# A hybrid encoder layer on one core: Hyena tiles read four and two ahead, output projection in fp16 parts

## The chip, the core and the metric

The kernel runs on one core of a Trainium2 chip. A core has a matrix engine (TensorE, PE in the profile), a vector engine (VectorE, DVE), a scalar engine (ScalarE, ACT), a general one (GpSimd, POOL) and an engine that issues most of the transfers here (SyncE, SP), each with its own instruction row, worked off in order. An instruction waits until those it depends on have signalled, and everything behind it on its engine waits with it. Working memory on the chip is SBUF (128 partitions); TensorE writes its results to PSUM, from which the other engines take them. The metric is the time of one launch in microseconds on the device; smaller is better.

## What is computed

One layer over two inputs, a prompt of 512 rows and a sample of 2048 rows, each row 1024 wide: 2560 rows, or 20 chunks of 128 rows. A normalised input is projected by `w_in`; three groups of heads (mLSTM, retention, Hyena) give 512 columns each; the 1536 mixed columns are projected back by `w_out` and added to the input, and a last RMSNorm follows.

```python
u = jnp.einsum('bld,de->ble', rmsnorm(x, norm_g[layer]), w_in[layer])
y_ml = mlstm_branch(...)       # 4 heads, both directions, chunks of 128
y_rt = retention_branch(...)   # 4 heads, both directions
y_hy = hyena_branch(...)       # z = x1*long_conv(v); z = x2*long_conv(z); z*silu(hy_z)
mixed = jnp.concatenate([y_ml, y_rt, y_hy], axis=-1)
x = x + jnp.einsum('ble,ed->bld', mixed, w_out[layer])
return rmsnorm(x, final_g)
```

`long_conv` is a convolution over the whole length through an FFT of twice the length; in the kernel each FFT is two rounds of small matmuls with a pass through memory between.

## The kernel before

The program has five stages in time. First a front part (normalisation, the Hyena projections). Then two streams that are merged: the Hyena stream, and a stream of the other input projections followed by retention. Then mLSTM, four heads, each in blocks of 512 rows. Then the output projection with the final norm.

**The merge.** `merge` takes generators with a total cost each and lets the one run next that has the smallest share of its cost done. A step yields its cost, and through `lag` also how much of the other stream's work has to pass before its own next step. A scheduler reorders on each engine what the generators emit, by its own estimate of times; the order that results is fixed when the kernel is built.

**The Hyena stream** is `stage_a0`, `freq(0)`, `inv_a(0)`, `freq(1)`, `inv_a(1)`. Tiles are 128 x 512 float32, 256 KB, from a pool of 18 buffers (`hb`). `stage_a0` loads `X` tiles two ahead and multiplies them (L921). `inv_a` works through 20 tiles twice: `load` brings two tiles of `Z`, `load_x` brings `X` (and for the second order `hyg`, a gate), `mid` multiplies `Z` (L1028), DVE multiplies by `X` (L1029), and for the second order POOL multiplies by the gate (L1033) and SP writes the result to `ymix` (L1036), the buffer of the mixed columns in memory. Per turn the order is `mid` of tile i, `X` of tile i+1, `Z` of tile i+2.

**The projections** of the other stream and of mLSTM are L554 and L544: fp16 matmuls, since `split_w` has scaled each weight matrix by a power of two (`scale_w`: a maximum on DVE, L348; a tiny matmul for the maximum over partitions, L358; a few small DVE steps) and cut it into a high and a low fp16 part (ACT L526, DVE L527).

**The output projection** works on two parts as well, but in float32r: `split` (L369 on ACT, L370 on DVE) cuts a tensor into a rounded part and the rest. The 1536 rows of `w_out` come in six groups of 256 rows (`load_wout`, L1211, two buffers); `split_wout` cuts one group and loads the next. Groups 0 to 3 are cut in the blocks of mLSTM's last head (`block_left`). `out_product` (L1287) makes 72 matmuls of 128 x 512 per row chunk: 12 column blocks, three products (high by high, high by low, low by high), two halves of the output. `turn_mixed` transposes the activations first (L1275, 12 transposes into three PSUM tiles, each split by L369 and L370). The first row chunk is done early: `early_load` reads its mixed columns, and `early_rows` runs beside the last mLSTM block, with groups 4 and 5 cut at steps 1 and 6 of its product. `final` then does chunks 1 to 19: product with the next chunk's transposes in its middle (step 5 of 12), addition of the input (L1343), square sum (L1350 on ACT), power (L1352 on POOL), scaling (L1354), store. The last block's own matmuls are L1438 and L1534 to L1539.

## Time and profile before

| what | value |
|---|---|
| median of three runs | 2651.07 us (2650.94 to 2654.84) |
| the profiled execution | 2648.68 us |
| its span, first to last instruction | 2646.9 us |
| granted TensorE clock, mean | 0.988 |
| TensorE (PE) busy | 2557.2 us, 97% |
| VectorE (DVE) busy | 1338.3 us, 51% |
| ScalarE (ACT) busy | 1053.7 us, 40% |
| GpSimd (POOL) busy | 493.9 us, 19% |
| moved by DMA | 321.30 MB, 121 GB/s over the span |
| chain that ended last | PE 78%, DMA 6%, ACT 4%, DVE 4% |

The share of busy time is an average over stages; where TensorE is busy all the time, only its own work counts, and where it waits, the thing it waits for. The clock is 1 where TensorE runs at 2.4 GHz and 0.5 where it runs at 1.2 GHz.

### The profile page before, as it was taken

To read this page: it belongs to the slowest core of one execution; us is meant where nothing else is said; L and a number is where in the kernel's file an instruction comes from. 1 tells how busy PE (TensorE), PEld (TensorE's weight loads), DVE (VectorE), ACT (ScalarE), POOL (GpSimd) and SP (SyncE) were. 2 spreads that over 40 slices of the span, in tenths; PEclk is the share of its full clock that TensorE was granted. 3 is DMA by queue.
4 is the path that set the end of the run, shared out by engine and by line. 5 is a ranking of instruction groups with operands and counts; after the bars stand their busy time and mean duration, and the time that the engine had idled before them with its cause. 6 is when DMAs were issued, how large, how long until landed. Compare 5 with 4: busy or idle time off the path is not lost.

```text
span 2646.9 us, 45607 instructions
## 1 busy us (share of the span) xinstructions
PE 2557.2 (97%) x17830; PEld 1770.2 (67%) x17830; DVE 1338.3 (51%) x3070; ACT 1053.7 (40%) x2030; POOL 493.9 (19%) x647
## 2 busy tenths in 40 slices
PE   7999979999999999999999979999999999899998
PEld 5565543444446777777777747787887777788887
DVE  6875635665554434545444444565556645522222
ACT  6455646442233333423333323555445545411111
POOL 0103312331011122322232341111111111100000
PEclk9999989999999999999999989999999999999999
DMA  6233377564454665434333782222121322322331
GB/s 207 84 99 108 98 220 252 167 187 127 126 160 128 207 198 160 126 100 132 116 104 97 226 228 65 52 66 61 37 64 42 89 73 59 133 102 95 111 104 48
DMA packets 238049, 321.30 MB, mean 121 GB/s; under 512 B 22755, under 2 KB 125947, under 8 KB 237833
## 3 DMA queue, kind: packets, MB, share of 16 engines
q1 hardware_dynamic: 237752, 318.11, 39.8%
q8 instruction: 141, 2.31, 0.4%
q14 instruction: 76, 0.61, 0.1%
q0 software_dynamic: 80, 0.26, 0.0%
HBM read 205.41 MB, written 112.89 MB: 120 GB/s over the span
## 4 chain that ended last, share of the span: by engine, by line
PE 78%; DMA 6%; ACT 4%; DVE 4%; issue 1%; SPq 1%; POOL 1%; DVEq 0%; POOLq 0%; ACTq 0%
PE ps L554 27%; PE ps L544 13%; PE ps L1287 13%; PE ps L948 6%; DMA rb<-rowd 3%; PE ps L983 3%; PE ps L1028 2%; PE ps L921 1%; PE ps L1639 1%; DMA wraw<-in_w_in 1%; PE ps L693 1%; PE ps L1438 1%; PE ps L1275 1%; PE ps L1698 1%; PE ps L846 1%
## 5 line engine op out<-in xcount | busy, mean ns | idle before, releaser
L554 PE MATMUL ps<-whi,h 128*128 128x256 f16 (+2 forms) x6080 | 913.7, 256 | 0.0
L554 PEld LDWEIGHTS <-h 128*128 128x128 f16 x9120 | 776.0, 98 | 150.0 <-issue 69.5
L554 PE MATMUL ps<-wlo,h 128*128 128x256 f16 (+2 forms) x3040 | 734.6, 256 | 0.0
L544 PE MATMUL ps<-h,whi 128*128 128x512 f16 x1600 | 484.9, 383 | 4.0 <-ACT whi L526 4.0
L544 PE MATMUL ps<-h,wlo 128*128 128x512 f16 x800 | 305.0, 381 | 0.0
L544 PEld LDWEIGHTS <-whi 128*128 128x128 f16 x1600 | 151.1, 99 | 212.8 <-issue 63.0
L1287 PE MATMUL ps<-h,yh 128*128 128x512 f32 x760 | 210.6, 396 | 1.6 <-ACT yh L369 1.6
L948 PE MATMUL ps<-hb,cB 128*64 128x512 f32 x640 | 165.9, 605 | 0.2 <-DMA hb<-F 0.2
L1287 PEld LDWEIGHTS ps<-h,yh 128*128 128x128 f32 x760 | 141.6, 188 | 33.7 <-ACT yh L369 1.9
L668 POOL TENSOR_TENSOR acc<-acc,win 128x512 f32<-128x512 f32 x80 | 107.2, 1340 | 201.4 <-ACT win L667 196.2
L544 PEld LDWEIGHTS <-wlo 128*128 128x128 f16 x800 | 78.7, 98 | 94.7 <-issue 4.9
L1618 POOL TENSOR_TENSOR m<-raw,tb 128x256 f32<-128x256 f32 x80 | 72.3, 904 | 336.2 <-ACT raw L1615 273.2
L1287 PE MATMUL ps<-h,yl 128*128 128x512 f32 x380 | 120.9, 395 | 0.0
L1615 ACT ACTIVATE raw<-ps,winv 128x256 f32<-128x256 f32 x80 | 37.8, 473 | 167.5 <-PE ps L554 98.9
L662 DVE TENSOR_TENSOR f<-ps,win 128x512 f32<-128x512 f32 x80 | 55.0, 688 | 88.7 <-PE ps L378 66.1
L813 DVE SCALAR_TENSOR_TENSOR cv<-u,sw,cv 128x512 f32<-128x512 f32 x120 | 98.1, 838 | 1.1
L527 DVE SCALAR_TENSOR_TENSOR wlo<-wraw,wsc,whi 128x512 f16<-128x512 f32 (+2 forms) x116 | 82.6, 749 | 22.8 <-ACT whi L526 21.6
L1637 ACT ACTIVATE vw<-va,rtv 128x128 f32<-128x128 f32 x144 | 51.9, 398 | 100.4 <-PE ps L1639 100.0
L948 PEld LDWEIGHTS ps<-hb,cB 128*64 128x64 f32 x640 | 41.5, 136 | 73.2 <-issue 60.6
L348 DVE TENSOR_REDUCE wam<-wraw 128x1 f32<-128x2048 f32 (+2 forms) x29 | 60.0, 2069 | 60.0 <-DMA wraw<-in_w_in 60.0
L1343 DVE TENSOR_TENSOR xt<-xt,ps 128x512 f32<-128x512 f32 x40 | 25.8, 684 | 126.9 <-PE ps L1287 126.9
L971 POOL TENSOR_TENSOR hb<-hb,hb 128x512 f32<-128x512 f32 x40 | 50.9, 1273 | 185.5 <-DVE hb L970 176.3
(318 smaller groups left out, 4045.8 us busy)
## 6 DMA issues: line engine op xcount, KB each, us to landing
F<-fo SPq DMA_DIRECT2D x160, 128.0 KB, 2.4
Sg<-hb SPq DMA_DIRECT2D x80, 256.0 KB, 2.3
hb<-F SPq DMA_DIRECT2D x80, 256.0 KB, 4.3
hb<-Sg SPq DMA_DIRECT2D x80, 256.0 KB, 5.1
Z<-hb SPq DMA_DIRECT2D x80, 256.0 KB, 3.5
hb<-Z SPq DMA_DIRECT2D x80, 256.0 KB, 3.7
rb<-rowd SPq DMA_DIRECT2D x80, 256.0 KB, 5.1
wraw<-in_w_in SPq DMA_DIRECT2D x36, 512.0 KB, 5.8
```

The lines of the kernel that those rows point to most:

```text
L348: self.nc.vector.tensor_reduce(am[:, 0:1], src, axis=AX.XY if len(src.shape) == 3 else AX.X, op=ALU.max, apply_absolute_value=True)
L527: v = nc.vector.scalar_tensor_tensor(lo[:, k], raw[:, k], s, hi[:, k], op0=ALU.mult, op1=ALU.subtract)
L544: nc.tensor.matmul(out, w[x][:, k, wc:wc + 128], self.hT[b][y][:, k], start=(k == 0 and i == 0), stop=(k == 7 and i == 2))
L554: nc.tensor.matmul(out, self.hT[b][x][:, k, c * 128:(c + 1) * 128], w[y][:, k, wc:wc + n], start=(k == 0 and i == 0), stop=(k == 7 and i = ...
L662: nc.vector.tensor_tensor(out=f, in0=ps, in1=win, op=ALU.mult)
L668: nc.gpsimd.tensor_tensor(out=acc, in0=acc, in1=win, op=ALU.add)
L813: nc.vector.scalar_tensor_tensor(d, u[:, t:t + 512], w(t), d, op0=ALU.mult, op1=ALU.add)
L948: nc.tensor.matmul(ps[half[h]], Cs[i][:, 128 * h + 64 * r:128 * h + 64 * r + 64], src[h], start=True, stop=True)
L983: nc.tensor.matmul(pz[h], c[half[h], 256 + 128 * r:384 + 128 * r], y[r][half[h]], start=(r == 0), stop=(r == 1))
L1028: nc.tensor.matmul(ps[64 * h:64 * h + 64], self.ai[L][:, 128:192], z[h], start=True, stop=True)
L1287: self.nc.tensor.matmul(self.pss[n], a[p], w[q][:, n * 512:(n + 1) * 512], start=(k == 0 and i == 0), stop=(k == 11 and i == 2))
L1618: nc.gpsimd.tensor_tensor(out=m, in0=raw[:, :, ::-1], in1=sin[:, c:c + 2], op=ALU.mult)
```

## The change

In the Hyena stream `stage_a0` loads four tiles ahead instead of two; `inv_a` loads both `Z` and `X` (and the gate) two tiles ahead, and per turn does `mid` first, then the loads, then for the first order `back`. The yielded costs and lags are others, and the stream's share in the merge is 295 instead of 275.

In the output projection both operands become fp16 parts. Each weight group gets a power-of-two scale (`scale_w`) and is cut in two instructions of 128 x 2048; the inverse scales are kept in `wog`. Per row chunk `mixed_parts` finds for each row the largest value times the inverse scale over the six column groups, makes a power-of-two factor of it, and cuts the activations into two fp16 parts in 12 instructions of 256 columns, before the transposes. `turn_mixed` then makes 24 fp16 transposes and copies three PSUM tiles of 128 x 1024. The addition of the input multiplies the product by the row's inverse factor. Groups 4 and 5 are cut in `early_load`. In `final` the parts of the next chunk are made at step 0 of the product, its transposes stand at step 8.

```diff
-                    self.drain(self.merge((self.chain(self.stage_a0(), self.freq(0), self.inv_a(0), self.freq(1), self.inv_a(1)), 275 * W3),
+                    self.drain(self.merge((self.chain(self.stage_a0(), self.freq(0), self.inv_a(0), self.freq(1), self.inv_a(1)), 295 * W3),
...
+        self.ident16 = self.T(cp, [128, 128], "ident16", F16)
+        nc.vector.tensor_copy(self.ident16, self.ident)
...
             st[i] = self.hx(0, L, j)
 
         n = len(seq)
-        load(0)
-        load(1)
-        for i in range(n + 1):
-            if i:
-                L, j = seq[i - 1]
-                self.stage_a(L, 0, j, st.pop(i - 1))
-            if i + 2 < n:
-                load(i + 2)
-            yield self.lag(0.86, 1.5)
+        for i in range(4):
+            load(i)
+        yield self.lag(0.0, 9.0)
+        for i in range(n):
+            L, j = seq[i]
+            self.stage_a(L, 0, j, st.pop(i))
+            if i + 4 < n:
+                load(i + 4)
+            yield self.lag(1.0, 0.5)
 
...
             self.stage_a(L, 1, j, st.pop(i))
 
         n = len(seq)
-        load(0)
-        yield self.lag(0.0, 5.0)
-        for i in range(-1, n + 1):
+        for i in range(2):
+            load(i)
+            load_x(i)
+        yield self.lag(0.0, 7.0)
+        for i in range(n + 1):
+            if i < n:
+                mid(i)
+            if i + 2 < n:
+                load(i + 2)
+                load_x(i + 2)
             if o == 0 and i >= 1:
                 back(i - 1)
-            if 0 <= i < n:
-                mid(i)
-            if i + 1 < n:
-                load_x(i + 1)
-            if i + 2 < n:
-                load(i + 2)
-            yield self.lag(1.71 if o == 0 else 0.86, LI)
+            yield self.lag(1.0 if o else 2.0, 1.5)
 
...
 
     def split_wout(self, i, hi, lo):
 
-        for k in range(2):
-            self.split(hi[k], lo[k], self.wraw[:, k])
+        nc = self.nc
+        if i == 0:
+            self.wog = self.T(self.cp, [128, 6], "wog")
+        s, inv = self.scale_w(self.wp, self.wraw)
+        nc.vector.tensor_copy(self.wog[:, i:i + 1], inv)
+        nc.scalar.activation(hi, self.wraw, AF.Copy, scale=s)
+        nc.vector.scalar_tensor_tensor(lo, self.wraw, s, hi, op0=ALU.mult, op1=ALU.subtract)
         self.wout[i] = hi, lo
         self.load_wout(i + 1)
 
     def block_left(self, h, b):
 
         if h == 3:
-            hi, lo = (self.T(self.hp, [128, 2, D], "h", F32R, bufs=10) for _ in range(2))
+            hi, lo = (self.T(self.hp, [128, 4, D], "h", F16, bufs=10)[:, 0:2] for _ in range(2))
             if b == 0:
                 self.load_wout(0)
-            self.split_next = lambda: self.split_wout(b, *([x[:, k] for k in range(2)] for x in (hi, lo)))
+            self.split_next = lambda: self.split_wout(b, hi, lo)
             if b < 4:
                 self.split_next()
 
...
         self.want(*MlHead.first_w(0))
         self.flush()
 
-    def turn_mixed(self, yt, yh, yl):
-
-        for y, hi, lo in zip(yt, yh, yl):
-            ps = self.ps()
-            for i in range(4):
-                self.nc.tensor.transpose(ps[:, i * 128:(i + 1) * 128], y[:, i * 128:(i + 1) * 128], self.ident)
-            self.split(hi, lo, ps)
-
-    def out_product(self, yh, yl, halves=((0, 1),)):
+    def mixed_parts(self, pool, yt, yp):
+
+        nc = self.nc
+        am = self.T(pool, [128, 8], "yam")
+        ie = self.T(pool, [128, 4], "yie", I32)
+        sc = self.T(pool, [128, 2], "ysc")
+        fs = self.T(pool, [128, 6], "yfs")
+        for q, y in enumerate(yt):
+            nc.vector.tensor_reduce(am[:, 2 * q:2 * q + 2], y.rearrange("p (g c) -> p g c", g=2), axis=AX.X, op=ALU.max, apply_absolute_value=True)
+        nc.vector.tensor_tensor(out=am[:, 0:6], in0=am[:, 0:6], in1=self.wog, op=ALU.mult)
+        nc.vector.tensor_reduce(am[:, 6:7], am[:, 0:6], axis=AX.X, op=ALU.max)
+        nc.vector.tensor_scalar(ie[:, 0:1], am[:, 6:7].bitcast(I32), 23, None, op0=ALU.logical_shift_right)
+        nc.vector.tensor_scalar(ie[:, 1:2], ie[:, 0:1], 15, 250, op0=ALU.max, op1=ALU.min)
+        nc.vector.tensor_scalar(ie[:, 2:3], ie[:, 1:2], -1, 268, op0=ALU.mult, op1=ALU.add)
+        nc.vector.tensor_scalar(ie[:, 3:4], ie[:, 1:2], -14, None, op0=ALU.add)
+        nc.vector.tensor_scalar(sc.bitcast(I32), ie[:, 2:4], 23, None, op0=ALU.logical_shift_left)
+        nc.vector.tensor_scalar(fs, self.wog, sc[:, 0:1], None, op0=ALU.mult)
+        for q, (y, p) in enumerate(zip(yt, yp)):
+            for g in range(2):
+                f, c = fs[:, 2 * q + g:2 * q + g + 1], slice(256 * g, 256 * g + 256)
+                nc.scalar.activation(p[:, 0, c], y[:, c], AF.Copy, scale=f)
+                nc.vector.scalar_tensor_tensor(p[:, 1, c], y[:, c], f, p[:, 0, c], op0=ALU.mult, op1=ALU.subtract)
+        return sc[:, 1:2]
+
+    def turn_mixed(self, parts, out):
+
+        nc = self.nc
+        for q, (y, o) in enumerate(zip(parts, out)):
+            ps = self.psum.tile([128, 2, 512], F16, tag="ps", name=self.nm("ps"))
+            for x in range(2):
+                for i in range(4):
+                    nc.tensor.transpose(ps[:, x, i * 128:(i + 1) * 128], y[:, x, i * 128:(i + 1) * 128], self.ident16)
+            if q == 1:
+                nc.vector.tensor_copy(o, ps)
+            else:
+                nc.scalar.activation(o, ps, AF.Copy)
+
+    def out_product(self, y, halves=((0, 1),)):
 
         self.pss = [self.ps(), self.ps()]
         for ns in halves:
             for k in range(12):
-                a = [y[k // 4][:, k % 4 * 128:(k % 4 + 1) * 128] for y in (yh, yl)]
-                w = [x[k % 2] for x in self.wout[k // 2]]
+                a = [y[k // 4][:, x, k % 4 * 128:(k % 4 + 1) * 128] for x in range(2)]
+                w = [x[:, k % 2] for x in self.wout[k // 2]]
                 for i, (p, q) in enumerate(((0, 0), (0, 1), (1, 0))):
                     for n in ns:
                         self.nc.tensor.matmul(self.pss[n], a[p], w[q][:, n * 512:(n + 1) * 512], start=(k == 0 and i == 0), stop=(k == 11 and i == 2))
...
         self.early = [self.T(ml, [128, 514], "ukT", bufs=3)[:, 0:512] for _ in range(3)]
         for i, y in enumerate(self.early):
             self.nc.sync.dma_start(y, self.ymix[0:128, 512 * i:512 * i + 512])
+        self.split_next()
+        self.split_wout(5, *(self.T(self.wp, [128, 2, D], x, F16) for x in ("whi", "wlo")))
 
     def early_rows(self, ml):
-        yh, yl = ([self.T(ml, [128, 516], x, F32R, bufs=4)[:, 0:512] for _ in range(3)] for x in ("va", "Cb"))
-        self.turn_mixed(self.early, yh, yl)
+        yp, yt = ([self.T(ml, [128, 1032], x, F16, bufs=4)[:, 0:1024].rearrange("p (x c) -> p x c", x=2) for _ in range(3)] for x in ("va", "Cb"))
+        self.early_inv = self.mixed_parts(self.cp, self.early, yp)
+        yield self.lag(0.0, 6.0)
+        self.turn_mixed(yp, yt)
         yield 1.3
-        for i, c in enumerate(self.out_product(yh, yl)):
-            if i == 1:
-                self.split_next()
-            if i == 6:
-                self.split_wout(5, *([self.T(self.wp, [128, D], x, F32R) for _ in range(2)] for x in ("whi", "wlo")))
-            yield c
+        yield from self.out_product(yt)
 
     def final(self):
         nc, I, fin = self.nc, self.I, self.fin
         V, A, P = nc.vector, nc.scalar, nc.gpsimd
-        xts, ys = {}, {}
+        xts, ys, inv = {}, {}, {0: self.early_inv}
 
         def load(t):
             xsrc = I['x_prompt'][0][t * 128:(t + 1) * 128] if t < 4 else I['x_sample'][0][(t - 4) * 128:(t - 3) * 128]
...
             nc.sync.dma_start(xts[t], xsrc)
 
         def turn(t):
-            yt, yh, yl = ys[t], self.T(fin, [128, 1536], "yh", F32R), self.T(fin, [128, 1536], "yl", F32R)
-            ys[t] = [[y[:, 512 * q:512 * q + 512] for q in range(3)] for y in (yh, yl)]
-            self.turn_mixed([yt[:, 512 * q:512 * q + 512] for q in range(3)], *ys[t])
+            yt, yp, yo = ys[t], self.T(fin, [128, 3, 2, 512], "yp", F16), self.T(fin, [128, 3, 2, 512], "yo", F16)
+            parts = [yp[:, q] for q in range(3)]
+            inv[t] = self.mixed_parts(fin, [yt.rearrange("p (q c) -> p q c", q=3)[:, q] for q in range(3)], parts)
+            ys[t] = parts, [yo[:, q] for q in range(3)]
+
+        def turned(t):
+            self.turn_mixed(*ys[t])
+            ys[t] = ys[t][1]
 
         load(1)
         load(0)
         fg = self.T(fin, [128, D], "fg", bufs=1)
         nc.sync.dma_start(fg, I['final_g'].unsqueeze(0).to_broadcast([128, D]))
         turn(1)
+        turned(1)
         for t in range(NCH):
             last = t == NCH - 1
             if t:
-                for i, _ in enumerate(self.out_product(*ys.pop(t), halves=((0,), (1,)) if last else ((0, 1),))):
-                    if i == 5 and t + 1 < NCH:
+                for i, _ in enumerate(self.out_product(ys.pop(t), halves=((0,), (1,)) if last else ((0, 1),))):
+                    if i == 0 and t + 1 < NCH:
                         turn(t + 1)
+                    if i == 8 and t + 1 < NCH:
+                        turned(t + 1)
             if t + 2 < NCH:
                 load(t + 2)
             dst = self.O['y0'][0][t * 128:(t + 1) * 128] if t < 4 else self.O['y1'][0][(t - 4) * 128:(t - 3) * 128]
...
             ss = self.T(fin, [128, 4], "ss")
             cols = [slice(n * 512, (n + 1) * 512) for n in range(2)]
             for o, ps in zip(cols, self.pss):
-                V.tensor_tensor(out=xt[:, o], in0=xt[:, o], in1=ps, op=ALU.add)
+                V.scalar_tensor_tensor(xt[:, o], ps, inv[t], xt[:, o], op0=ALU.mult, op1=ALU.add)
             sq = self.T(fin, [128, D], "sq", BF16)
             if last:
                 for n, o in enumerate(cols):
```

TensorE at the end of the last mLSTM block. Before, the early chunk's transposes and product (L1275, L1287; `h` weights, `va` and `Cb` the two activation parts) stand between output matmuls of the block (L1534 to L1539):

```order
L1539 MATMUL ps_25226<-Cb_24164,rb_25008 128x129
L1275 MATMUL ps_25256<-ident_63,ukT_25182 128x128 x4
L1275 MATMUL ps_25263<-ident_63,ukT_25183 128x128 x4
L1287 MATMUL ps_25270<-h_23753,va_25243 128x512
L1287 MATMUL ps_25271<-h_23753,va_25243 128x512
L1287 MATMUL ps_25270<-h_23754,va_25243 128x512
L1287 MATMUL ps_25271<-h_23754,va_25243 128x512
L1534 MATMUL ps_25296<-va_24047,t_4243_25013 128x129
```

After, lines are 41 to 44 higher here (L1578 to L1583, L1309, L1324):

```order
L1580 MATMUL ps_25374<-cf_25362,rb_25055 128x129
L1581 MATMUL ps_25374<-va_24061,t_4262_25069 128x129
L1583 MATMUL ps_25374<-Cb_24178,rb_25055 128x129
L1580 MATMUL ps_25391<-cf_25379,rb_25055 128x129
L1581 MATMUL ps_25391<-va_24061,t_4262_25069 128x129
L1309 LDWEIGHTS va_25324
L1309 MATMUL ps_25422<-ident_10_85,va_25324 128x128
L1309 LDWEIGHTS va_25324
```

All output matmuls of the block now stand ahead of the first transpose; behind these rows come the other transposes, 24 in all, and the 72 product matmuls of the early chunk in one piece.

DVE in the last stage, one chunk. Before (`yl` the low part, `xt` the input rows):

```order
L370 TENSOR_TENSOR yl_26610<-ps_26611,yh_26609 128x512
L370 TENSOR_TENSOR yl_26610<-ps_26618,yh_26609 128x512
L370 TENSOR_TENSOR yl_26610<-ps_26625,yh_26609 128x512
L1343 TENSOR_TENSOR xt_26450<-xt_26450,ps_26571 128x512
L1343 TENSOR_TENSOR xt_26450<-xt_26450,ps_26572 128x512
L1351 TENSOR_SCALAR ss_26672<-ss_26672 128x1
L1354 SCALAR_TENSOR_TENSOR xt_26450<-xt_26450,ss_26672,fg_25433 128x1024
```

After (`yam`, `yie`, `ysc`, `yfs` the row maxima and factors, `yp` the parts, `yo` the transposed parts):

```order
L1387 SCALAR_TENSOR_TENSOR xt_25599<-ps_25756,ysc_25622,xt_25599 128x512
L1387 SCALAR_TENSOR_TENSOR xt_25599<-ps_25757,ysc_25622,xt_25599 128x512
L1293 TENSOR_SCALAR ysc_25914<-yie_25913 128x2
L1294 TENSOR_SCALAR yfs_25915<-wog_23759,ysc_25914 128x6
L1395 TENSOR_SCALAR ss_25893<-ss_25893 128x1
L1299 SCALAR_TENSOR_TENSOR yp_25910<-yt_25889,yfs_25915,yp_25910 128x256
L1398 SCALAR_TENSOR_TENSOR xt_25599<-xt_25599,ss_25893,fg_25536 128x1024
L1299 SCALAR_TENSOR_TENSOR yp_25910<-yt_25889,yfs_25915,yp_25910 128x256 x5
L1286 TENSOR_REDUCE yam_26204<-yt_26181 128x2 x3
```

The three subtractions from PSUM have gone; between two chunks' additions there are now the maxima, the small steps, a copy and six differences, and the parts of the chunk after next stand behind the additions (L1387) of the present one.

SP in the last inverse Hyena step. Before (`Z`, `hyg` and `X` are loads, `ymix` is the write of a finished tile):

```order
L790 DMA hb_16472<-hyg_184 64x512 x2
L790 DMA hb_16475<-X_2048_59_183 64x512 x2
L1036 DMA ymix_177<-hb_16248 64x512 x2
L890 DMA hb_16478<-Z_1_68_192 128x512
L890 DMA hb_16480<-Z_1_68_192 128x512
L790 DMA hb_16515<-hyg_184 64x512 x2
L1036 DMA ymix_177<-hb_16327 64x512 x2
L790 DMA hb_16518<-X_2048_59_183 64x512 x2
```

After:

```order
L892 DMA hb_15376<-Z_1_69_194 128x512
L892 DMA hb_15378<-Z_1_69_194 128x512
L792 DMA hb_15380<-hyg_186 64x512 x2
L792 DMA hb_15383<-X_2048_60_185 64x512 x2
L1038 DMA ymix_179<-hb_15343 64x512 x2
L892 DMA hb_15414<-Z_1_69_194 128x512
L892 DMA hb_15416<-Z_1_69_194 128x512
L792 DMA hb_15418<-hyg_186 64x512 x2
L792 DMA hb_15421<-X_2048_60_185 64x512 x2
```

The write of a tile now stands ahead of all four loads for the tile two further on; before, the loads of the gate and of `X` came one tile ahead and those of `Z` two. On TensorE the second order's 40 matmuls (L1028, after the change L1030) all lie ahead of retention's last block, with some 350 projection matmuls behind them.

## Rows read from the trace of the kernel before

**Rows 1.** The page, part 4: shares of the span by line on the chain.

```profile
PE ps L554 27%; PE ps L544 13%; PE ps L1287 13%; PE ps L948 6%; DMA rb<-rowd 3%; PE ps L983 3%; PE ps L1028 2%; PE ps L921 1%; PE ps L1639 1%; DMA wraw<-in_w_in 1%; PE ps L693 1%; PE ps L1438 1%; PE ps L1275 1%; PE ps L1698 1%; PE ps L846 1
```

**Rows 2.** Chain in order of time, last stage: start us, length us, engine, output, line, count.

```profile
2308.38 16.72 PE ps L1287 x72
2325.10 1.31 PE ps L1275 x12
2326.41 16.71 PE ps L1287 x72
...
2614.60 25.08 PE ps L1287 x108
```

**Rows 3.** The same view in the mLSTM stage, 1645 to 1680.

```profile
1650.10 2.68 PE ps L554 x48
...
1668.10 5.19 PE ps L544 x24
```

**Rows 4.** Windows, last stage: length, busy us of PE, PEld, DVE, ACT, POOL; clock; DMA.

```profile
2400.00:2450.00 50.00, 50.00 (x230) 40.98 (x229) 12.15 (x19) 6.61 (x12) 1.62 (x3) 1.00 0.27 98
```

**Rows 5.** Groups of instructions by line and form, DVE: busy us, mean ns; idle before.

```profile
L348 DVE TENSOR_REDUCE wam<-wraw 128x1 f32<-128x2048 f32 x24 | 54.9, 2286 | 56.0 <-DMA wraw<-in_w_in 56.0
...
L370 DVE TENSOR_TENSOR yl<-ps,yh 128x512 fp32r<-128x512 f32 x57 | 35.9, 685 | 87.6 <-ACT yh L369 87.6
...
L1354 DVE SCALAR_TENSOR_TENSOR xt<-xt,ss,fg 128x1024 f32<-128x1024 f32 x19 | 24.4, 1285 | 13.6 <-POOL ss L1352 13.6
...
L527 DVE SCALAR_TENSOR_TENSOR wlo<-wraw,wsc,whi 128x256 f16<-128x256 f32 x16 | 7.1, 481 | 8.6 <-ACT whi L526 8.6
...
L1351 DVE TENSOR_SCALAR ss<-ss 128x1 f32<-128x1 f32 x20 | 3.1, 154 | 24.9 <-ACT sq L1350 24.9
```

**Rows 6.** The same view, ACT.

```profile
L1615 ACT ACTIVATE raw<-ps,winv 128x256 f32<-128x256 f32 x80 | 37.8, 473 | 167.5 <-PE ps L554 98.9 <-issue 49.1 <-POOL hb L971 9.1
...
L369 ACT ACTIVATE yh<-ps 128x512 fp32r<-128x512 f32 x57 | 29.9, 598 | 115.6 <-PE ps L1275 115.6
...
L1350 ACT ACTIVATE sq<-xt 128x1024 bf16<-128x1024 f32 x19 | 20.1, 1058 | 160.1 <-DVE xt L1343 160.1
```

**Rows 7.** Timeline of PE, last mLSTM block: start us, length, instruction [idle before, releaser].

```profile
2272.86 2.07 PE L1287 MATMUL ps<-h,va 128*128 128x512 f32 x4 [4.36 <-ACT va L369]
...
2298.45 1.19 PE L1287 MATMUL ps<-h,yh 128*128 128x512 f32 x4 [1.63 <-ACT yh L369]
```

**Rows 8.** Timeline of ACT, same place.

```profile
2261.84 1.06 ACT L369 ACTIVATE whi<-wraw 128x1024 fp32r<-128x1024 f32 x1 [0.96 <-DMA wraw<-in_w_out]
```

**Rows 9.** Windows around the last mLSTM block, columns as in rows 4.

```profile
2250.00:2260.00 10.00, 10.00 (x93) 9.18 (x92) 9.72 (x28) 5.56 (x10) 4.30 (x3) 1.00 0.54 116
...
2270.00:2280.00 10.00, 7.14 (x23) 6.05 (x24) 5.71 (x24) 4.88 (x12) 2.27 (x2) 0.66 0.00 0
```

**Rows 10.** Windows over the last inverse Hyena step.

```profile
1470.00:1545.00 75.00, 75.00 (x597) 57.87 (x595) 38.51 (x84) 25.44 (x64) 35.32 (x30) 1.00 0.87 251
1545.00:1595.00 50.00, 34.59 (x143) 15.26 (x142) 19.94 (x51) 5.73 (x13) 18.43 (x24) 0.83 0.67 190
```

**Rows 11.** Waits of PE, 1470 to 1595: waiting line, releaser: us, times, longest.

```profile
PE ps L1028 <- DMA hb<-Z: 11.1, 3, 4.8
```

**Rows 12.** Timeline of SP's DMA issues for one tile of that step.

```profile
1555.23 1.10 SPq L1036 DMA_DIRECT2D ymix<-hb  x2
1556.43 1.19 SPq L790 DMA_DIRECT2D hb<-X  x2
1557.72 1.00 SPq L890 DMA_DIRECT2D hb<-Z  x2
1558.81 1.09 SPq L790 DMA_DIRECT2D hb<-hyg  x2
```

**Rows 13.** Timeline of PE at the Hyena stream's start.

```profile
367.07 3.78 PE L921 MATMUL ps<-hb,ai 64*128 64x512 f32 x8 [8.14 <-DMA hb<-X]
```

**Rows 14.** One window of the middle, columns as in rows 4.

```profile
800.00:900.00 100.00, 100.00 (x753) 71.29 (x753) 38.65 (x89) 30.21 (x62) 18.85 (x19) 1.00 0.53 161
```

## Prediction

> **What bounds the kernel now.** I read the page's chain first: TensorE carries it, and three lines carry TensorE, the two projection lines L554 and L544 and the output product L1287 with 13% [rows 1]. Then the chain in order of time in the last stage: 72 matmuls of L1287 in 16.71 us, 12 transposes of L1275 in 1.31 us, and nothing between; one row chunk takes 18.02 us (2308.38 to 2326.41) [rows 2]. So in that stage only the price of these 84 instructions counts; DVE is busy 12.15 and ACT 6.61 of 50 us [rows 4]. The middle of the program is as full: 100.00 of 100 us [rows 14], where another order of the same work is worth nothing. I then looked for places where TensorE waits, since only there can the Hyena part of the change pay: 8.14 us for X at the start of the Hyena stream [rows 13], and the end of that stream, 1545 to 1595, where TensorE is busy 34.59 of 50 us at a granted clock of 0.83 [rows 10]. The third place is the junction from the last mLSTM block to the early row chunk [rows 7 to 9].
>
> The profiled run took 2648.68 us, 1.78 more than its span of 2646.9 and 2.39 less than the median of 2651.07. I sum changes to the span and set them against the median. A change under 0.2% (5.3 us) cannot be told from none here.
>
> **Steady final stage: −19.9 us.** A float32 matmul of L1287 costs 16.71 / 72 = 0.2321 us. The same width in fp16 is on the chain elsewhere: 24 of L544 in 5.19 us, 0.2163 each [rows 3]. So 72 take 15.57 us, 1.14 less. The 12 transposes become 24 in fp16; 48 fp16 matmuls of 128 columns took 2.68 us, 0.0558 each [rows 3], so 24 take 1.34, against 1.31 for twelve now. The upper bound is the price of today's transposes, 0.109 each, 2.62 us. I take 1.34, since rows 3 are fp16 with one weight load each, as here. Period 15.57 + 1.34 = 16.91 instead of 18.02. From 2316.7 (the end of chunk 1's product, half-way through the 72 matmuls that start at 2308.38) to 2639.68 lie 323.0 us now, and 17 × 16.91 + 15.57 = 303.0 after.
>
> What is added per chunk runs on DVE and ACT. DVE: three maxima over 512 columns (a quarter of 2.286 each, 1.7), some eight steps at 0.154 (1.2), six differences of 256 columns at 0.481 (2.9), a copy of 1024 columns (about 1.3), less three subtractions of 0.685 (2.1): 5 us on top of about 4.4 (12.15 × 18.02 / 50) [rows 4, 5]. ACT: six parts at 0.473 and two copies of about 1.06, less three splits of 0.6 [rows 6]. Both stay far under 16.9. The latency counts too: the order puts chunk t+1's parts behind the additions of chunk t−1, which wait for that product's end. From there two additions of 512 columns from PSUM, at the 0.685 of L370, 1.06 for the square, 1.29 for the last scaling, six parts 2.9 and small steps are about 8 us; the transposes stand behind 54 matmuls, 11.7 us in. Cover 3.7 us; were it gone, each missing us would be paid 17 times.
>
> The Trainium skill, "TensorE: Matmul & The Clock Gate", section "Back-to-back issue gap", speaks against that price: in a stream of weight loads and matmuls, 128 columns sustain about 81 ns each. By that 24 transposes would take 1.94 us, an estimate from that page, and 10 us of the gain would go. The trace does not agree: rows 3 are such a stream, at 56 ns.
>
> **Junction: +14 us (3 to 22).** Now the early product starts at 2272.86, is mixed with the last block's output matmuls, and chunk 1's product starts at 2298.45 [rows 7]. The order after has all output matmuls first, then 24 transposes, then 72 product matmuls in a row: what filled the waits of the block now stands ahead of a longer DVE chain, and the early transposes wait for the scales of all six weight groups. Group 5's load lands at 2261.84 [rows 8], its buffer being freed by group 3's split. DVE, busy 9.72 of 10 us there [rows 9], has by then another maximum of 2.29 to do, so I put the landing at 2264. Then: maximum 2.3, about 5 for the block's own rows and scale steps that stand between, 2.1 for ACT's high part of 2048 columns, two differences of 2048 columns at 2.6 (twice L1354's 1.285), a dozen steps 1.8, first parts 0.47 + 0.96, transposes and a copy 1.06: 2283 [rows 5, 6]. TensorE is idle for most of that and starts cold; at 0.66 of 7.14 busy us [rows 9] that cost 2.4 now. Product 15.6 + 2.4: 2301. Then DVE's row has the additions of chunk 0 ahead of the parts of chunk 1: 1.4 + 1.2 + 1.3, maxima of chunk 2 1.7, parts 2.9, small steps 0.9; TensorE waits about 10 us, and runs chunk 1's product with chunk 2's transposes in 15.6 + 1.3 + 2.4, to 2330. Against 2316.7 that is +14. Low end: group 5 lands as now and the block's rows slip in beside ACT, start 2278, second wait 6. High end: both waits 4 us longer.
>
> The first four weight groups each cost DVE a maximum of 2.3 and two differences' more, about 4 us, in a head whose DVE has room; TensorE now has a tiny matmul per group that waits for the maximum, with output matmuls queued behind it. I take +1 (0 to 4).
>
> **Hyena's end: +2 us (−10 to +14).** Lost now: 50 − 34.59 = 15.4 idle and 34.59 × 0.17 = 5.9 for the clock, 21 us, of which 11.1 are three waits for Z [rows 10, 11]. After, some 350 projection matmuls, about 36 us, and retention stand behind the last Hyena matmul, so that loss goes. But the twenty tiles of the last inverse step then stand in about 75 us of TensorE work instead of 100 (what the order puts between the first and the last of them, at the rows' prices), 3.75 us per tile. A tile moves 5 × 256 KB, 1.31 MB; in 1470 to 1545 the queues gave 251 GB/s at a share of 0.87 [rows 10], so full queues give 290, 4.5 us per tile. SP alone needs 1.10 + 1.19 + 1.00 + 1.09 = 4.4 us to issue one [rows 12], and its write of a result, which waits for POOL, stands ahead of the loads for two tiles on. I take 4.9 us per tile: 20 × (4.9 − 3.75) = 23 us of waits in place of 21. At 4.4, SP's own price, it would be 13 (−8); at 5.5, 35 (+14); reading further ahead takes up to two tiles' time off either.
>
> **Hyena's start: 0 us (−4 to +1).** Loads for four tiles go out before the first matmul, but in SP's order they stand where two stood, behind the same transfers; the wait of 8.14 us for X [rows 13] is for the first tile and stays.
>
> Sum: −19.9 + 14 + 1 + 2 + 0 = −3, so 2651 − 3 = 2648.
>
> **Rivals.**
> (1) The read-ahead hides Hyena's end. For it: deeper read-ahead lets transfers run while retention computes, and the share of 0.67 in 1545 to 1595 [rows 10] says that queues had room there. Against: 0.87 before it. The waits fall to a few us, −18 for that term instead of +2: 2628. It decides if a tile comes in 4 us or less.
> (2) The junction's chain is shorter than I add it up, since rows on DVE overlap waits I counted in series: +4 instead of +14, with the rest as forecast: 2638.
> (3) Slower: the tile loop of write, load, multiply is a latency chain. If a tile takes 5.5 us (SP's 4.4 and 1.1 for POOL's result), the twenty tiles make TensorE wait 35 us where 21 are lost now: +14 instead of +2, 2660. It decides above 5.1 us per tile. For it: one engine issues everything; against: loads are two tiles ahead.
> (4) The fp16 transposes cost what today's cost, 2.62 us: 17 × 1.28 = 22 more, 2670. By the skill's 81 ns it would be 10 more, 2658.
>
> **How the numbers follow.** Forecast 0.40 (2648; its own range 2643 to 2656), (1) 0.20, (2) 0.15, (3) 0.15, (4) 0.06 by rows and 0.04 by the page's price. Range 2627 to 2663: it leaves out part of (1), the far price of (4) and the sums of two bad ends. Faster by over 0.2%: (1), (2) and a little of the forecast, 0.37. Same: the rest of the forecast, 0.37. Slower: (3), (4) and a tail, 0.26.
>
> **What would show it.** In the profile after: a chunk's period of 16.91 us (15.57 + 1.34) on the chain; DVE about 28 of 50 us in the last stage; the early product's first matmul near 2283 less what came before, in one unbroken run, and a second wait of about 10 us between it and chunk 1; waits of TensorE for Z from some 1460 on, about 1 us per tile, and none in the last 30 us of retention. Wrong: a period over 17.5 (transposes, or DVE's parts late); the early product still mixed with outputs; no waits for Z at all, which is (1), or gaps of 2 us per tile, which is (3).

## The result and the profile after

The changed kernel takes 2690.76 us (median of four runs, 2685.74 to 2697.68) beside 2651.01 for the kernel before: a ratio of 1.015, interval 1.0122 to 1.0178. It is 40 us slower, where I had forecast 2648 and no measurable change. Its profiled span is 2692.0 us, 45.1 more than the 2646.9 before.

Four places make up the 45 us; each is read off as the time at which the same point of the program is passed. First the start of mLSTM. These two lines are the view of one source line, TensorE's transposes of mLSTM's keys, in the kernel before and after; the two times in them are those of the first and the last of these transposes.

```profile
L1410 PE MATMUL ps<-ident,kT x80: 272/273/332, 1600.7 to 2178.9; 128*128 128x128 f32 x80
```

```profile
L1454 PE MATMUL ps<-ident,kT x80: 272/273/477, 1636.0 to 2223.4; 128*128 128x128 f32 x80
```

mLSTM starts at 1636.0 instead of 1600.7, **35.3 us later**. Next the junction, on the chain in order of time after (start, length, what):

```profile
2306.98 2.64 DVE h L1224
2309.65 4.99 DMA wraw<-in_w_out
2314.66 2.30 DVE wam L350
...
2337.52 17.63 PE ps L1324 x71
...
2363.78 4.50 DMA yt<-ymix
2368.31 1.87 DVE yam L1286 x3
...
2371.63 22.19 PE ps L1324 x102
2393.82 1.34 PE ps L1309 x24
```

Of the 102 matmuls that start at 2371.63, 48 end chunk 1's product: 2371.63 + 48 × 0.216 = 2382.0. Before it was 2316.7 [rows 2], so 65.3 us have been lost by then, 30.0 of them since mLSTM's start. By the two lines above **9.2** of the 30.0 are lost inside mLSTM's heads (587.4 us from the first transpose to the last, where 578.2 were), and **20.8** behind them, at the junction. From there the last stage gives **20.3** back. The same view of its end:

```profile
2630.14 1.34 PE ps L1309 x24
2631.48 15.54 PE ps L1324 x72
2647.02 1.34 PE ps L1309 x24
...
2665.24 19.44 PE ps L1324 x90
```

A chunk has a period of 15.54 + 1.34 = 16.88 us, against 18.02 [rows 2]: 72 fp16 matmuls at 0.216, and 24 transposes in 1.34, which is 56 ns each. From 2382.0 to the last matmul's end at 2684.68 lie 302.7 us, where 323.0 were.

Most of the 35.3 us are lost at the end of the Hyena stream. Some 8 are gone by 1440, before its last step: 4584 projection matmuls have started by then, 120 fewer than before, at 0.109 us each, against 20 more records of the Hyena stream at 0.257. `fp16_alone` below, whose Hyena stream is that of before, is some 5 us behind there too. Then the stretch from 1440 to mLSTM's start, before and after (columns as in rows 4):

```profile
1440.00:1600.70 160.70, 144.03 (x1058) 101.26 (x1054) 76.22 (x179) 41.29 (x101) 64.07 (x64) 0.95 0.70 202
```

```profile
1440.00:1636.00 196.00, 172.19 (x1175) 117.38 (x1172) 72.87 (x194) 43.43 (x107) 63.89 (x65) 0.93 0.55 157
```

TensorE is idle for 23.8 us there instead of 16.7. Two windows of it, after:

```profile
1475.00:1550.00 75.00, 64.36 (x331) 33.48 (x329) 19.58 (x44) 9.47 (x24) 23.55 (x20) 0.93 0.80 233
1600.00:1635.00 35.00, 28.26 (x243) 22.60 (x240) 15.85 (x51) 10.16 (x25) 8.11 (x17) 0.90 0.18 52
```

While the twenty last tiles run, TensorE is busy 64.36 of 75 us, which looks like a mild loss. But it starts 331 matmuls in that time (by the profile's records), where the kernel before started 597 in 75 us [rows 10], and of the projections 227 instead of 395. The busy share hides part of this because the two matmuls of a tile, each for one half of the output (L1028, after L1030; two records each), now mostly stand apart in TensorE's order. First a tile before, then one after:

```profile
1471.17 1.08 PE L1028 MATMUL ps<-hb,ai 128*64 128x512 f32 x4
```

```profile
1479.60 1.07 PE L1030 MATMUL ps<-hb,ai 128*64 128x512 f32 x2
1480.61 0.28 PE L556 MATMUL ps<-whi,h 128*128 128x256 f16 x1
...
1482.02 1.07 PE L1030 MATMUL ps<-hb,ai 128*64 128x512 f32 x2
```

Side by side both take 1.08 us, apart each takes 1.07. In the last step 26 of the 40 stand alone, 7 before, and none in `after_lag` below; all the 160 records of this line keep TensorE busy for 66.8, 52.1 and 44.3 us in these three (a lower clock is in these numbers too). No run shows how much of this TensorE would otherwise have spent waiting. The second row is retention finishing alone after the last tile: 28.26 of 35 us at a clock of 0.90. TensorE's waits for Z from 1440 to 1640, after, are the same as before in kind [rows 11], but there are more of them, 16.0 us in all instead of 11.1:

```profile
PE ps L1030 <- DMA hb<-Z: 16.0, 8, 3.7
```

### The profile page after: what moved, and what is told of

It is laid out like the page before. It is cut to its first block, busy times and chain, and to the rows that moved or that the text cites. A ratio compares the mean times of both kernels' runs of the same rounds, so it can differ in the third digit from the quotient of the medians.

```text
span 2692.0 us, 46524 instructions
## 1 busy us (share of the span) xinstructions
PE 2577.9 (96%) x18082; PEld 1656.6 (62%) x18082; DVE 1439.1 (53%) x3413; ACT 1110.4 (41%) x2124; POOL 495.1 (18%) x647
## 4 chain that ended last, share of the span: by engine, by line
PE 39%; DMA 5%; DVE 4%; ACT 2%; issue 1%; POOL 1%; SPq 1%; DVEq 0%; POOLq 0%; ACTq 0%
PE ps L556 14%; PE ps L1324 11%; PE ps L546 5%; DMA rb<-rowd 3%; PE ps L1030 1%; DMA wraw<-in_w_in 1%; PE ps L1482 1%; DMA hb<-Z 1%; PE ps L1309 1%; PE ps L1554 1%; PE ps L950 1%; DVE t L1510 1%; PE ps L1578 1%; PE ps L1683 1%; PE ps L1580 0%
## 5 line engine op out<-in xcount | busy, mean ns | idle before, releaser
L1324 PE MATMUL ps<-h,yo 128*128 128x512 f16 x1140 | 254.3, 381 | 1.5 <-ACT yo L1313 1.2
L1324 PEld LDWEIGHTS <-yo 128*128 128x128 f16 x1368 | 133.3, 98 | 160.0 <-issue 2.5
L350 DVE TENSOR_REDUCE wam<-wraw 128x1 f32<-128x2048 f32 (+2 forms) x35 | 73.7, 2105 | 62.3 <-DMA wraw<-in_w_in 57.9
L813 DVE TENSOR_SCALAR cv<-u,sw 128x512 f32<-128x512 f32 x60 | 34.9, 581 | 109.5 <-ACT u L802 93.7
L1313 ACT ACTIVATE yo<-ps 128x1024 f16<-128x1024 f16 x38 | 37.1, 1022 | 125.5 <-PE ps L1309 125.5
L658 ACT ACTIVATE win<-dl,tneg 128x512 f32<-128x512 f32 x80 | 57.6, 723 | 61.6 <-POOL acc L670 55.2
```

Source lines behind the costliest of these rows:

```text
L350: self.nc.vector.tensor_reduce(am[:, 0:1], src, axis=AX.XY if len(src.shape) == 3 else AX.X, op=ALU.max, apply_absolute_value=True)
L658: nc.scalar.activation(win, dl, AF.Exp, scale=tneg[:, jt:jt + 1])
L1324: self.nc.tensor.matmul(self.pss[n], a[p], w[q][:, n * 512:(n + 1) * 512], start=(k == 0 and i == 0), stop=(k == 11 and i == 2))
```

## The experiments

Theories at this point: A, the Hyena half costs the time, and the fp16 half nearly pays its own junction; B, the longer vector work of the fp16 half is at fault all through the mLSTM heads. Within the Hyena half: C, SP's row of loads and writes is a loop of waits; D, the queues carry no more.

**Each half alone.** `hyena_alone` is the kernel before with the three Hyena edits, `fp16_alone` the changed kernel without them.

> The kernel before with the Hyena half of the change alone (loads four and two tiles ahead, share 295); output projection as before. Theory A (the loss of the changed kernel sits at the end of the Hyena stream: mLSTM starts 35 us later, at 1636.0 instead of 1600.7): the time before plus 33 to 38 us, about 2687, mLSTM starting near 1636. Theory B (the loss comes mostly from the longer vector work of the fp16 half): within 10 us of before, 2645 to 2660.

> The changed kernel with the Hyena half undone. Theory A: minus 20 us in the last stage, plus about 15 at the junction, plus about 10 to 15 in the mLSTM heads (weight groups cut with a maximum and longer differences): 2655 to 2662, chunk period 16.88. Theory B: the slow part stays here, 2680 and more. A third reading (the 10 to 15 us in the mLSTM heads follow from the later start and not from the weight groups): about 2646.

Measured: 2687.86 us (ratio 1.0145, 1.0129 to 1.0162), and 2654.73 (1.0016, 1.0006 to 1.0026). Theory A holds: plus 38 and plus 5 us beside the kernel before in the same rounds (2649.86). The key transposes of mLSTM, first with the Hyena half and then with the fp16 half:

```profile
L1411 PE MATMUL ps<-ident,kT x80: 272/273/475, 1633.1 to 2217.9; 128*128 128x128 f32 x80
```

```profile
L1453 PE MATMUL ps<-ident,kT x80: 272/273/476, 1603.3 to 2183.3; 128*128 128x128 f32 x80
```

So the fp16 half alone starts mLSTM at 1603.3, and the 10 to 15 us that I expected in the heads for cutting the weight groups did not come: 580.0 us beside 578.2 before. The longer heads go with the Hyena half, 584.8 us, and not with a late start: they take 585.0 in `after_lag` below, which starts mLSTM earlier than the kernel before. Their cause stays open. The junction of the fp16 half on the chain reads so:

```profile
2266.86 2.64 DVE h L1223
2269.52 4.94 DMA wraw<-in_w_out
2274.49 2.30 DVE wam L350
...
2288.09 2.23 DVE wlo L1223
...
2297.33 17.76 PE ps L1323 x71
...
2323.70 4.70 DMA yt<-ymix
...
2331.74 13.34 PE ps L1323 x61
```

Group 3's difference ends at 2269.5 and only then may group 5's load go, which lands at 2274.5; the maximum, two differences and the parts follow, and the early product starts at 2297.33, where it had started at 2272.86 [rows 7]. Chunk 1's product ends at 2331.74 + 48 × 0.216 = 2342.1, 25.4 later than before. Of these 2.6 are there at mLSTM's start, 1.8 come in its heads and 21.0 at the junction, the same as in the changed kernel. In the last stage all but 5 us come back.

**The write's place in SP's row.** In the changed kernel a tile's write stands behind the loads of one further tile, and waits for POOL. `after_late_write` issues it a turn later, behind that turn's loads (first cut); in its trace the loads of three further tiles stand ahead of a write, not of two as the expectation has it. `after_act_write` gives the write to ACT (second cut).

```diff
-                for h in range(2):
-                    nc.sync.dma_start(rows[h], g[64 * h:64 * h + 64])
+                st[i] = self.half_rows(self.ymix[:, 1024:1536], L, j), g
...
+            if i >= 1:
+                (write if o else back)(i - 1)
```

```diff
-                    nc.sync.dma_start(rows[h], g[64 * h:64 * h + 64])
+                    nc.scalar.dma_start(rows[h], g[64 * h:64 * h + 64])
```

> The changed kernel, with the write of a finished Hyena tile issued one turn later, so that on SP the loads of two further tiles stand ahead of it instead of one. Theory C (SP's row is the loop: it waits for POOL's result of a tile whose loads it issued only one tile ago, and the loads behind it start late): a tile falls from about 5.6 us to 4.4 to 4.8 (SP's own price or the queues'), the twenty tiles take 90 to 96 us instead of 112, and the time falls by 12 to 20 us to about 2675. Theory D (the queues' throughput, 1.31 MB a tile at 230 to 290 GB/s, sets the pace): no change, within 4 us.

> The changed kernel, with the writes of finished Hyena tiles issued by ACT instead of SP: SP has only loads in its row there (3.3 us per tile). Theory C: as with the later write or better, a tile at 4 to 4.5 us, minus 15 to 25 us, unless ACT's waits for POOL hold up retention's own ACT work, which would show as waits of TensorE for ACT. Theory D: within 4 us of the changed kernel.

Measured: 2677.88 and 2679.14 us, 13 and 12 less than the changed kernel. From the first tile to the last the pace went from 5.90 us (1445.1 to 1557.2, 19 tiles) to 5.33 and 5.60. So C is true in part: the wait in SP's row costs 0.57 us a tile by the later write and 0.30 by ACT's. The pace stays far from 4.4, SP's own price [rows 12].

**Two issuing engines.** `after_two_queues` is the late write with the gate's and X's loads issued by ACT.

> The changed kernel with the later write, and the gate's and X's loads of the last inverse step issued by ACT instead of SP; the bytes are the same. Theory S (SP's issues, 4.4 us a tile, and its waits set the pace): a tile falls from 5.2 us to 4.6 or less, the time to 2662 to 2670. Theory Q (the queues' throughput at this mix of packets, 1.31 MB per tile at some 250 GB/s): a tile stays at 5.0 to 5.4, the time within 5 us of the later write's 2678.

Measured: 2680.36 us, a pace of 5.36. This is what theory Q expects. The window over the tiles, first with SP alone (late write), then with two issuers; the last columns are the clock, the DMA engines' share and GB/s:

```profile
1445.00:1540.00 95.00, 84.59 (x469) 46.61 (x469) 30.05 (x72) 13.90 (x36) 34.49 (x30) 0.96 0.89 256
```

```profile
1445.00:1540.00 95.00, 80.47 (x442) 43.85 (x441) 35.12 (x73) 13.08 (x35) 35.06 (x31) 0.92 0.92 265
```

The share is 0.89 and 0.92 and the rate 256 and 265 GB/s: the transfers themselves nearly fill the time. The Trainium skill, "DMA: Bandwidth & Descriptors", section "Issuing engines are not separate DMA queues", says that transfers started by different engines run on the same 16 DMA engines, and that more issuers save only issuing time; these rows agree. What ACT's issues cost retention shows as waits of TensorE for ACT, 7.6 us in two.

**The turn, the share, the lag.** `after_old_inv` has the old turn of `inv_a` back (order of loads, costs, lag), `after_share275` only the old share; `after_lag` changes one number of the changed kernel, which holds for both inverse steps: LI is 4.2. No run has the four tiles of read-ahead alone.

```diff
-            yield self.lag(1.0 if o else 2.0, 1.5)
+            yield self.lag(1.0 if o else 2.0, LI)
```

> The changed kernel with the inverse step's turn (order of loads, costs, lags) as before; four tiles ahead in the first step and the share of 295 stay. On TensorE its twenty last tiles then lie in about 100 us of work instead of 62 (counted from the order at the prices of the trace), and 20 us of other work are left behind the last of them instead of 50. Theory E (a tile takes SP and the queues 5 to 6 us whatever the order, and what counts is how much TensorE work lies beside each tile and behind the last): most of the 35 us come back, 2655 to 2665. Theory F (the larger share alone, which brings the Hyena work forward, costs the time): no gain, 2680 to 2692.

> The changed kernel with the share of 275 instead of 295, read-ahead as in the change. The last twenty tiles lie in about 56 us of TensorE work, as dense as in the change (62), but only 12 us of other work stand between the last of them and mLSTM instead of 55. Theory E: the loop still takes 5.2 to 5.8 us per tile, 105 to 115 us, so TensorE waits as long there; what retention loses alone at its end (about 15 us) comes back: 2675 to 2690. Theory F: back to the old pace, 2655 to 2662.

> The changed kernel with one number changed: the lag of a turn of the inverse step is 4.2 again instead of 1.5; the new order of loads, the costs and the share stay. The last twenty tiles then lie in 102 us of TensorE work instead of 62 and 14 us stand behind them before mLSTM. Theory E (the work beside each tile decides, not the order of the loads): like the run with the whole old turn, 2640 to 2650. Rival (the new order of loads, each tile's write ahead of the loads two further on, is what costs): within 10 us of the changed kernel.

Measured: 2644.41 (0.9971, 0.9959 to 0.9983), 2686.96 (1.0141, 1.0126 to 1.0156), 2644.35 us (0.9971, 0.9958 to 0.9985). This settles what costs the 35 us: the lag of 1.5. The share alone changes little: tiles as dense as in the change, a pace of 5.80, TensorE waiting 16.6 us for Z. The lag alone gives back all of it and more, with the new order of loads and the larger share in place. Its window over the tiles, to be held against the first window of the changed kernel above:

```profile
1475.00:1550.00 75.00, 74.79 (x604) 57.84 (x602) 37.92 (x89) 26.69 (x67) 36.69 (x32) 1.00 0.84 249
```

604 matmuls start instead of 331, at nearly the same rate of transfers, 249 GB/s beside 233. The tiles come no faster, 6.35 us each; but the order now puts enough of the other stream's work between two of them, and TensorE is full. My expectation of 2655 to 2665 for the old turn was too careful: with the old turn or the old lag mLSTM starts at 1587, 16 us earlier than in `fp16_alone`, and 10 us of that are left at the end. What these runs have beyond `fp16_alone` is the share of 295 and the read-ahead of the first step; which of the two brings it was not tried.

**The junction.** `fp16_packed` puts both parts of a weight group in one buffer (the change had used half of each of two), so that two groups are cut in each of the first three blocks of the last head, with two loads under way. `fp16_packed_order` also keeps chunk 0's additions behind chunk 1's parts on DVE.

```diff
-            hi, lo = (self.T(self.hp, [128, 4, D], "h", F16, bufs=10)[:, 0:2] for _ in range(2))
...
+        if h == 3 and b < 3:
...
+            for i in (2 * b, 2 * b + 1):
+                x = self.T(self.hp, [128, 4, D], "h", F16, bufs=10)
+                self.split_wout(i, x[:, 0:2], x[:, 2:4])
...
+                a = V.scalar_tensor_tensor(xt[:, o], ps, inv[t], xt[:, o], op0=ALU.mult, op1=ALU.add)
+                if t == 0:
+                    self.tc.keep_in_program_order(a)
```

> The fp16 half alone, with the two parts of a weight group packed in one buffer instead of two, so that two groups are cut in each of the first three blocks of the last mLSTM head and none is left for the end. Theory G (the early product waits for group 5's load and its chain on VectorE): the first early product matmul moves from 2297.3 to about 2285, where the block's output matmuls end; the second wait of 16.6 us stays: 2640 to 2646. Rival: the cutting has only moved, the earlier blocks wait for it instead: 2652 to 2656.

> The same, and on VectorE the additions of chunk 0 are held behind the parts of chunk 1 that stand before them in the program. Theory H (the second wait, 16.6 us between the early product's end and chunk 1's product, is chunk 1's parts queued behind chunk 0's additions): that wait falls to under 3 us, 13 us less than with the packing alone: 2627 to 2633, 18 to 24 below the kernel before. Rival: the load of chunk 1's mixed columns, issued late by SP, is what is waited for: within 4 us of the packing alone.

Measured: 2637.54 (0.9955, 0.9938 to 0.9973) and 2629.55 us (0.9923, 0.9908 to 0.9939). The early product starts at 2283.9 in the first, as expected, 13 us earlier than in `fp16_alone`:

```profile
2283.94 15.48 PE ps L1325 x71
...
2308.05 6.00 DMA yt<-ymix
...
2317.39 22.19 PE ps L1325 x102
```

In the second the transposes of chunk 1 follow the early product with a wait of 0.19 us (timeline of TensorE), and the chain is TensorE's again three microseconds later:

```profile
2298.24 2.80 PE L1310 MATMUL ps<-ident,yp 128*128 128x128 f16 x24 [0.19 <-ACT yp L1299]
```

```profile
2301.15 12.47 PE ps L1325 x57
2313.62 1.34 PE ps L1310 x24
2314.96 14.89 PE ps L1325 x69
```

That brought 8 us and not the 13 I expected: part of the second wait had been filled with 24 matmuls of chunk 1 already.

**Both repairs.** `old_inv_packed` and `lag_packed` are `after_old_inv` and `after_lag` with packing and order.

> The old turn of the inverse step, the share of 295 and four tiles ahead in the first step, with the packed weight parts and the additions held behind chunk 1's parts. If the two repairs add up: 2644 less the 25 us that packing and order gave the fp16 half, 2617 to 2624, faster than both kernels by over 1%. If the gain of the old turn and that of the junction overlap (one stage's waits only move into the next): 2625 to 2632.

> The changed kernel with the lag of 4.2 and the packed weight parts with the additions held back. By theory E and adding up: 2615 to 2625, within 6 us of the old turn's; if the new order of loads costs something of its own, above that by what it costs.

Measured: 2614.88 us (0.9863, 0.9838 to 0.9887) and 2614.13 (0.9857, 0.9828 to 0.9886). The gains add up, with 4 to 5 us more than the sum, whose place I have not looked for. `lag_packed` computes all that the changed kernel does and is faster than it by 77 us and than the kernel before by 38.

## Why the prediction was wrong

**Steady last stage: right.** 302.7 us against 303.0 forecast, period 16.88 against 16.91. The rows of fp16 matmuls elsewhere in the trace priced both the product and the transposes; the bound by today's transposes was not needed. The Trainium skill, "TensorE: Matmul & The Clock Gate", section "Back-to-back issue gap", has 81 ns for 128 columns in a stream of weight loads and matmuls; the row of 24 in 1.34 us does not agree, at 56. DVE's copy was cheaper (0.68 for 1024 columns, not 1.3) and its maxima dearer (0.68 for 512, not 0.57); both stayed under cover.

**Junction: right in kind, two thirds of the size.** I had forecast 14 us at the junction and 1 in the heads. At the junction 20.8 came in the changed kernel and 21.0 in the fp16 half alone. The second wait, which I had at about 10 us, was right: from the end of the early product at 2315.1 to the end of chunk 1's product at 2342.1, 27 us passed for 16.9 of work. The step that failed is group 5's landing. I moved it from 2261.84 [rows 8] by 2 us, for one more maximum; in `fp16_alone` it moved by 12.6, of which 4.4 are there already at the last key transpose (2183.3 instead of 2178.9). The load waits for the difference of group 3, which waits in DVE's row, and DVE was full there [rows 9]; how much each of the maxima and longer differences ahead of it adds was not taken apart. The packing shows that the landing was the term: with the load out of the way the early product's start fell by 13 us. The 9.2 us in the heads of the changed kernel were in no term of mine beyond the +1; most of them go with the Hyena half (6.6 in `hyena_alone`).

**Hyena's end: the term that was missed.** Forecast +2, range −10 to +14; measured 35 at mLSTM's start. The sum was 20 × (price of a tile − TensorE work beside it), and its direction held in the runs: with little work beside a tile (the change, `after_share275`) TensorE loses time, with much (`after_lag`) it does not. Four things in it failed.
- The price of a tile: I took 4.9 us, 5.5 at worst, a little above SP's 4.4 [rows 12] and the 4.5 of queues at 290 GB/s, which I had got by dividing the rate by the share [rows 10]. The DMA engines reach such a rate where loads stand close (314 GB/s at a share of 0.99 from 860 to 880, after), but this step keeps them at no such share: 256 and 265 GB/s at 0.89 and 0.92 are the best of a whole step. Measured 5.90, so by the sum's own form 20 × 1.0 = 20 us more. The trace of before held it, the tiles there took 5.9 too (1471.2 to 1583.6, 19 tiles); I ascribed that to a lack of read-ahead.
- The work beside a tile: I took 75 us for the twenty; my later count, in the expectation of `after_old_inv`, is 62, 3.1 a tile instead of 3.75. By the sum's form that is 13 us more.
- Retention left alone: I had let the old loss go and put nothing in its place. The row 1600 to 1635 above has 6.7 us of idle time and 28.26 × 0.10 = 2.8 of clock.
- I took the loss to be waits, and these were less than the 23 us that I had: 16.0 us for Z in place of 11.1. The rest of the loss is a lower clock and the two matmuls of a tile standing apart, which no term held.

The stream's start, 370.5 instead of 367.07 [rows 13], is not the change's: it is 371.2 in `fp16_alone`, without the Hyena edits, and 365.6 in `after_lag`, with them.

With the 2 forecast the first three make 44.6, more than the 35.3 measured, although some 8 of these are lost before the last step begins. So the terms are right in kind and are not shown one by one. What the runs show is the whole: the lag alone moves mLSTM's start from 1636.0 to 1586.4.

**Rivals.** (1), the read-ahead hides the end, fell by the same measurement: the pace of no run came under 5.3 us a tile. (3) had the direction and a pace above its 5.1 us, but the time came out 30 us above its 2660, and its mechanism was there only in part: the chain of waits through SP accounts for 0.6 us of a tile (late write), and the 5.33 that are left stand with transfers that nearly fill the time, which I had not put into it. (2) and (4) fell: the junction was longer, the transposes cheap.

**The chances.** Slower had 0.26 and the range ended at 2663. The bounds of the Hyena term were too narrow since both ends were added up from prices of single issues and waits; a bound from the pace of the kernel before (6 us per tile with 3.75 us of work beside it) would have given 45 us of waits and put slower first.

## What to carry to other kernels

A number that spaces one stream's steps among another's work is worth what the steps take in the resource that they share, here 5.3 to 5.9 us a tile where TensorE waited for them; setting it closer moved the work away from under the transfers, and neither the read-ahead of the change, nor a later write, nor a second issuing engine made up for it. Price such a step by the pace at which it ran when it was the bound, not by its bytes over a rate that the trace does not show in that step. And where work moves in front of a chain at the end of a stage, look for the buffer whose release starts the last load: here the load landed 12.6 us later. Last, compare a trace with those of other variants before an early offset is put down to the change: the 3.4 us at the stream's start were there in a kernel without it.

## What the runs showed of the hardware that I had not expected

- TensorE's busy share can stand at 64.36 of 75 us with 331 matmuls started where 604 started in another run; here the count of instructions per window told the loss, and the share did not.
- Two float32 matmuls for 64 output partitions each, side by side in TensorE's order, took 1.08 us together, and 1.07 us each when other work stood between them.
- The 16 DMA engines, on this mix of transfers of 128 and 256 KB, gave 256 to 265 GB/s over 95 us at shares of 0.89 to 0.92, with one engine issuing or two.
- An fp16 transpose of 128 x 128 costs 56 ns in a run of 24, half of a float32 one (1.31 us for 12 [rows 2]).
